# Decoder layer in Winograd's seven products: sums of weight blocks made in other stages

## The chip, the cores and the metric

The kernel runs on one core of a Trainium2 chip. The metric is the time of one execution in microseconds (us) on the device; the kernel before was timed three times.

## The reference

One layer on a residual stream `h` of 1024 tokens by 1024 channels, float32, with `D_FF` = 2816:

```python
f = (silu(n(h) @ w_gate) * (n(h) @ w_up)) @ w_down      # FFN1
h = h + 0.5 * n(f)
z = n(h) @ w_in                                          # u | v | c | ga | gb, 1024 columns each
a = gelu(u) * spatial(layernorm(gelu(v)))                # 128-token chunks, 4 groups
b = pool_mixer(c)                                        # trailing means over 2, 4, 8, 16 tokens
y = sigmoid(ga) * (a @ w_out_a) + sigmoid(gb) * (b @ w_out_b)
h = h + n(y @ w_o)
h = h + 0.5 * n(FFN2(n(h)))                              # like FFN1
h = h + n(sigmoid(n(h) @ ple_w_gate) * (p @ ple_w_proj))
```

`n` is an RMSNorm with a gain of its own at each place.

## The kernel before

Every large product is done in Winograd's form of Strassen's scheme: each operand is cut into 2 by 2 blocks, and seven block products replace eight. They come in the order p1, p2, p5, p6, p3, p7, p4 (`ORDER`), which the text numbers 0 to 6. p1 and p2 use plain blocks of the right operand (the weights), p3 too; p5, p6, p7 and p4 use sums of its blocks (b11+b12 and three more). Each float32 operand is split into a rounded high part (ScalarE, L148) and the rest (VectorE, L149), and three matmuls of 128x512 make one float32 product (L156 to L158). TensorE (PE) therefore works through a fixed list of matmuls, with VectorE (DVE) and ScalarE (ACT) splitting, adding and reading out beside it.

The stages are: projection of p; FFN1 gate and up ("hidden", 11 column groups, `Columns`); FFN1 down (`ffn_down`); v (`Rows`); u and c (`Columns`, 4 groups); the gates with the pool mixer; the products with w_out_a and w_out_b; the product with w_o (`Rows`); FFN2 hidden; FFN2 down; the ple product. A right operand either makes its sums when they are wanted (`from_blocks`, L152: VectorE adds of 128x1024 in `raw` tiles) or reads sums that an earlier stage left in DRAM (`from_stored`).

A down stage has for each of its seven products six steps, written (i, kp) with i the product and kp 0 to 5: five of two 128-row chunks and one of a single chunk, 24 matmuls per full step. A step loads two `raw` tiles of 512 KB and splits them into an `X` tile; loads run three steps ahead. At the end of a product each of four PSUM banks is read out (`outs[t].read`), and from product 4 on `closing` turns the finished tokens into the next stage's left operand: multiply by the gain (L742), add the residual (L754), normalise (L179), transpose on TensorE (L233), split and add (L208 to L216). Tokens come in eight tiles; the transposes of tiles 4 to 7 (T4 to T7 in the text) stand among the first matmuls of the next stage.

Steps that are not urgent wait in `later`, a queue sorted by a key: each readout allows it some us of work. The tile framework then fixes one order of instructions per engine, which the chip keeps; loads and stores of all kinds go through the one queue of SyncE (SP), in order, and an issue whose buffer is not free holds up all behind it. Tile pools that matter: `raw` 6, `f` (`full`) 11, `X` 7, `wt` 4 buffers of 128x1024 or larger.

Before the change, `weight_sums` gives six steps to FFN1 down as `beside`: the sums of w_out_a (two halves), w_out_b (two) and w_o (two). One half is four loads of 512 KB into `f` tiles, four adds of 128x1024 (L152) and four stores (`store_sums`, L416). They are entered in this line of `ffn_down`:

```python
if beside and (kp == 1 or (i, kp) == (0, 3)):
    beside.pop(0)()
```

FFN1 hidden has `row_sums` of the v columns of `w_in` beside groups 3 to 6, FFN2 hidden those of `ple_w_gate`: per quarter two loads of 512 KB, four adds of 128x512, four stores of 256 KB. FFN2 hidden makes its own weight sums for all 11 groups; groups 0 and 1 lead (`lead` 2), so that p1 and p2 of both come before p5 of group 0.

Of the kernel before, what the change touches and what calls it, by code (L numbers as in the profile page):

```python
# [13 lines left out]
P = 128  # L14
T = 1024
D = 1024
# [4 lines left out]
HC = NC // 2  # L21
HT = 512
# [61 lines left out]
def layer_kernel(ctx: ExitStack, tc: tile.TileContext, a: dict, out: bass.AP):  # L84
    nc = tc.nc
    x, p = a["x"][0], a["p"][0, 0]
# [13 lines left out]
    later = Later()  # L100
# [12 lines left out]
    def full(shape=(D,), dt=F32):  # L113

        return fp.tile([P, *shape], dt, name="f", tag="f")
# [11 lines left out]
    def scratch(name, n, w=D):  # L127
        return [dr.tile([P, w], F32, name=f"{name}{i}", tag=f"{name}{i}") for i in range(n)]
# [3 lines left out]
    ga_d, gb_d, y_d = (dr.tile([P, KD, T], F32, name=s, tag=s) for s in ("ga_d", "gb_d", "y_d"))  # L132
    as_d, bs_d = (scratch(s, 7, KD // 2 * HT) for s in ("a_s", "b_s"))

    tr_d = {s: [scratch(f"{s}_t{h}", 4) for h in range(2)] for s in ("w_v", "ple_w_gate")}
    tw_d = {s: [scratch(f"{s}_t{h}", 4) for h in range(2)] for s in ("w_out_a", "w_out_b", "w_o")}
    ws_d = dr.tile([P, HT], F32, name="ws_d", tag="ws_d")
    sv_d = dr.tile([P, KD, T], F32, name="sv_d", tag="sv_d")
    s_d = {s: scratch(f"{s}_s", 7, HC * HT) for s in ("ffn1", "ffn2")}
    t_d = {s: {i: scratch(f"{s}_t{i}", 1, HC * HT)[0] for i in (2, 3, 5, 6)} for s in ("ffn1", "ffn2")}  # L140
# [10 lines left out]
    def add(dst, u, v, e=nc.vector):  # L151
        e.tensor_tensor(dst, u, v, op=ALU.add)  # L152
# [213 lines left out]
    def from_blocks(block, put):  # L366


        def each(u, v):
            for x, y in zip(u, v):  # L370
                add(x, x, y, nc.vector)

        def make(i, st, keep):
            name = ORDER[i][0]
            if name in ("p1", "p2"):
                b = block(i, 0)
                if keep[i]:
                    st[("11", "21")[i]] = b
                return put(b)
            if name == "p5":  # L380
                st["11"] = st.get("11") or block(0, 0)
                st["12"] = block(0, 1)
                each(st["11"], st["12"])
                return put(st["11"])
            if name == "p6":
                st["22"] = block(1, 1)
                each(st["11"], st["22"])
                return put(st["11"])
            if name == "p3":
                return put(st["22"])  # L390
            if name == "p7":
                each(st["12"], st["22"])
                return put(st["12"])
            each(st["11"], st.get("21") or block(1, 0))
            return put(st["11"])

        return make

    def from_stored(block, put, sums):


        def make(i, st, keep):
            where = {"p1": (0, 0), "p2": (1, 0), "p3": (1, 1)}
            name = ORDER[i][0]
            return put(block(*where[name]) if name in where else sums(("p5", "p6", "p7", "p4").index(name)))

        return make

    def store_sums(blocks, dst):

        b11, b12, b22, b21 = (full() for _ in range(4))
        for t, load in zip((b11, b12, b22, b21), blocks):
            load(t)
        for d, t, u, v in ((0, b11, b11, b12), (2, b12, b12, b22), (1, b22, b11, b22), (3, b21, b22, b21)):
            add(t, u, v)
            nc.sync.dma_start(dst[d], t)  # L416
# [4 lines left out]
    class Columns:  # L421
        def __init__(self, groups, blocks, lead, stored=None):


            self.lead = lead
            self.steps = [(g, i) for g in range(lead) for i in range(2)]
            self.steps += [(g, i) for g in range(groups) for i in range(2 if g < lead else 0, 7)]
            state = {}

            def make(step):  # L430
                g, i = step

                def block(r, c):
                    t = raw([4, 256])
                    (w0, *c0), (w1, *c1) = blocks(g)

                    def rows(w):
                        return w[r * HT:(r + 1) * HT, :].rearrange("(k p) f -> p k f", p=P)

                    if w0 is w1 and c1[c] == c0[c] + 1:  # L440
                        nc.sync.dma_start(t, rows(w0)[:, :, c0[c] * P:(c0[c] + 2) * P])
                    else:
                        for n, (w, b) in enumerate(((w0, c0[c]), (w1, c1[c]))):
                            nc.sync.dma_start(t[:, :, n * P:(n + 1) * P], rows(w)[:, :, b * P:(b + 1) * P])
                    return [t]

                def put(b):
                    w = wt([2, 4, 256])
                    split(w[:, 0], w[:, 1], b[0])
                    return w  # L450

                def sums(j):
                    t = raw([4, 256])
                    nc.sync.dma_start(t, stored[g][j].rearrange("p (k f) -> p k f", k=4))
                    return [t]

                f = from_stored(block, put, sums) if stored else from_blocks(block, put)
                return f(i, state.setdefault(g, {}), (g >= lead, g >= lead))

            self.right = Right(make, self.steps, lambda s: LOOK if s < 2 * lead - 1 else 3)  # L460
# [125 lines left out]
        later.add(0, 1.4, second)  # L586


    def hidden_weights(s):
        wg, wu = (a[f"{s}_w_{n}"][0] for n in ("gate", "up"))  # L590
        return Columns(HC, lambda c: ((wg, c, c + HC), (wu, c, c + HC)), 2)

    def row_sums(w, dst):

# [99 lines left out]
    def ffn_down(right, outs, last, beside=()):  # L694

        beside = list(beside)
        for i, (name, place, fresh) in enumerate(ORDER):
            if fresh:
                for t in range(4):
                    outs[t].b[place] = bank()  # L700
            def mm(t, o, k, first, last):
                cols = slice(t * P, (t + 1) * P)
                mm3(
                    outs[t].b[place], (o[:, 0, 0, k, cols], o[:, 0, 1, k, cols]),
                    (o[:, 1, 0, k, :], o[:, 1, 1, k, :]), fresh and first, last,
                )

            outer = PAIRS - TAIL
            for kp in range(outer):
                o, n = right.get(i * PAIRS + kp)  # L710
                for k in range(n):
                    for t in range(4):
                        mm(t, o, k, kp == 0 and k == 0, False)
                    later.allow(2.0)
                if beside and (kp == 1 or (i, kp) == (0, 3)):
                    beside.pop(0)()

            rest = [right.get(i * PAIRS + kp) for kp in range(outer, PAIRS)]
            if i == 6:
                last()  # L720
            for t in range(4):
                for j, (o, n) in enumerate(rest):
                    for k in range(n):
                        mm(t, o, k, False, j == TAIL - 1 and k == n - 1)
                outs[t].read(name)
                later.allow(2.0)
# [45 lines left out]

    w_in = a["w_in"][0]
    h1_cols = hidden_weights("ffn1")


# [51 lines left out]
    left = Seven()  # L828
# [15 lines left out]
    g = gain(a["ffn1_pre_g"][0])  # L844
# [5 lines left out]
    for j in range(2):  # L850
        for t in range(NT):
# [10 lines left out]
            if t % 2 == 1 and len(xs) < NT:  # L862
                n = len(xs)
# [3 lines left out]
    while len(xs) < NT:  # L867
        n = len(xs)
# [4 lines left out]

    def weight_sums():

        steps = []
        for s, dst in tw_d.items():
            w = a[s][0]
            for h in range(2):
                def blocks(w=w, h=h, by_columns=s != "w_o"):  # L880
                    def load(r, c):
                        if by_columns:
                            v = w[r * HT:(r + 1) * HT, c * HT + h * 256:c * HT + (h + 1) * 256]
                            k = 4
                        else:
                            v = w[r * HT + h * 256:r * HT + (h + 1) * 256, c * HT:(c + 1) * HT]
                            k = 2
                        return lambda t: nc.sync.dma_start(
                            t.rearrange("p (k f) -> p k f", k=k), v.rearrange("(k p) f -> p k f", p=P)
                        )  # L890

                    return [load(0, 0), load(0, 1), load(1, 1), load(1, 0)]

                steps.append(lambda blocks=blocks, d=dst[h]: store_sums(blocks(), d))
        return steps

    down = down_weights("ffn1")
    ffn_hidden("ffn1", left, h1_cols, lambda: down.ahead(3), row_sums(w_in[:, D:2 * D], tr_d["w_v"]))
    v_rows = Rows(w_in[:, D:2 * D], tr_d["w_v"])
    left = Seven()  # L900
    ffn_down(
# [100 lines left out]
        u_places, c_places = pairs(), pairs()  # L1002
        return [Out(u_final, u_places), Out(c_final, c_places)]

    uc_cols.run(left, uc_outs, lambda g: None, lambda i: gate_cols.right.ahead(2) if i == 6 else None, 5)
    later.flush()

    def col_pairs(s):
# [140 lines left out]
        if i < 2:  # L1149
            ysum.put(i, slice(2, 4), ALL, o)  # L1150

    o_rows = Rows(a["w_o"][0], tw_d["w_o"])

    def last_a(i):
        if i >= 2:
# [15 lines left out]
    later.add(0, 3.7, lambda: ysum.sums(slice(2, 4), ALL, *(tops[i] for i in range(4)), full((2, HT)), 1.3))  # L1171


    h2_cols = hidden_weights("ffn2")
    left = Seven()
    o_rows.run(
        ysum, closing(1.0, lambda t: h1_d[t], h2_d, "mix_post_g", "ffn2_pre_g", left),
# [86 lines left out]
```

## Time and profile before

| | us |
|---|---|
| three runs | 2123.2, 2124.75 (median), 2127.16 |
| the profiled execution, its own time | 2126.75 |
| its span, first to last instruction | 2125.0 |
| TensorE busy | 2064.4 (97% of the span) |
| VectorE, ScalarE, GpSimd busy | 1473.6, 939.2, 140.4 |

The span is almost all TensorE time, so the places to read are the few where TensorE stands still. In the rows below a timeline line gives the start, the length, engine, source line and operation, tiles written and read, the number of instructions merged, and in brackets the idle time before it and what ended it. A line number is one of the kernel before.

### The profile page before, as it was taken

How to read it: one execution, taken by the hardware profiler on the slowest of the kernel's cores; microseconds unless marked ns; L12 is line 12 of the kernel's file. 1: busy time of each engine (PE TensorE's matmuls, PEld its weight loads, DVE VectorE, ACT ScalarE, POOL GpSimd, SP SyncE). 2: the span in 40 equal slices, each digit the busy share in tenths (PEclk: the TensorE clock that was granted, in tenths of full speed). 3: DMA queues.
4: the chain of work that ended last, by engine and by line, in shares of the span. 5: the costliest groups of instructions: out<-in, count | busy, mean ns of one | idle time of the engine just before them, and what ended most of it. 6: DMA issues, size and time to landing. Idle time of an engine off the chain costs nothing. (4 is left out here: it accounts for less than half of the span.)

```text
span 2125.0 us, 25592 instructions
## 1 busy us (share of the span) xinstructions
PE 2064.4 (97%) x9228; PEld 1707.8 (80%) x9228; DVE 1473.6 (69%) x1789; ACT 939.2 (44%) x1360; POOL 140.4 (7%) x212
## 2 busy tenths in 40 slices
PE   7999999999999899999999999989999999999987
PEld 6888888888887788888788887768888888888876
DVE  6766677677657887568587758896666667454787
ACT  7533333344445643334455535653333334443664
POOL 2000000000011110000000002310000000000222
PEclk9999999999999999999999999999999999999999
DMA  8455756489859325535379985636366556764763
GB/s 292 125 172 174 245 175 217 146 310 405 309 196 346 125 82 179 178 129 182 129 261 363 315 255 204 197 104 208 129 222 234 183 186 233 249 205 146 263 237 129
DMA packets 306289, 448.42 MB, mean 211 GB/s; under 512 B 20593, under 2 KB 177265, under 8 KB 306161
## 3 DMA queue, kind: packets, MB, share of 16 engines
q1 hardware_dynamic: 305072, 444.68, 61.0%
q0 software_dynamic: 1088, 2.10, 0.6%
q8 instruction: 73, 1.20, 0.2%
q14 instruction: 56, 0.45, 0.1%
HBM read 301.21 MB, written 145.49 MB: 210 GB/s over the span
## 5 line engine op out<-in xcount | busy, mean ns | idle before, releaser
L156 PE MATMUL ps<-X,wt 128*128 128x512 f32 x1904 | 742.1, 390 | 2.8 <-DVE wt L149 1.7
L157 PE MATMUL ps<-X,wt 128*128 128x512 f32 x1904 | 742.1, 390 | 0.1
L158 PE MATMUL ps<-X,wt 128*128 128x512 f32 x1904 | 741.0, 390 | 0.0
L149 DVE TENSOR_TENSOR wt<-raw,wt 128x1024 fp32r<-128x1024 f32 x282 | 343.9, 1221 | 221.2 <-ACT wt L148 208.2
L156 PEld LDWEIGHTS ps<-X,wt 128*128 128x128 f32 x1904 | 358.6, 188 | 78.4 <-DVE wt L149 2.2
L158 PEld LDWEIGHTS ps<-X,wt 128*128 128x128 f32 x1904 | 358.2, 188 | 74.9
L157 PEld LDWEIGHTS ps<-X,wt 128*128 128x128 f32 x1904 | 358.5, 188 | 74.1 <-DVE X L149 0.4
L148 ACT CAST wt<-raw 128x1024 fp32r<-128x1024 f32 x282 | 295.6, 1049 | 261.9 <-PE ps L158 125.7
L149 DVE TENSOR_TENSOR X<-raw,X 128x1024 fp32r<-128x1024 f32 (+1 forms) x201 | 223.9, 1145 | 107.1 <-ACT X L148 106.6
L148 ACT CAST X<-raw 128x1024 fp32r<-128x1024 f32 (+1 forms) x201 | 191.8, 994 | 149.6 <-PE ps L158 77.3
L157 PE MATMUL ps<-X 128*128 128x512 f32 x616 | 241.4, 392 | 0.3 <-DVE X L149 0.3
L156 PE MATMUL ps<-X 128*128 128x512 f32 x616 | 237.3, 391 | 3.9 <-ACT X L148 2.7
L158 PE MATMUL ps<-X 128*128 128x512 f32 x616 | 240.0, 391 | 0.0
L152 DVE TENSOR_TENSOR raw<-raw 128x1024 f32<-128x1024 f32 x120 | 146.6, 1222 | 8.1 <-DMA raw<-in_ffn_w_up_dram 3.6
L156 PEld LDWEIGHTS ps<-X 128*128 128x128 f32 x616 | 116.0, 188 | 28.6 <-ACT X L148 3.1
L157 PEld LDWEIGHTS ps<-X 128*128 128x128 f32 x616 | 116.3, 189 | 24.9 <-DVE X L149 0.8
L158 PEld LDWEIGHTS ps<-X 128*128 128x128 f32 x616 | 116.3, 189 | 23.9
L157 PE MATMUL ps<-wt,X 128*128 128x512 f32 x336 | 132.6, 395 | 1.2 <-DVE wt L149 1.2
L158 PE MATMUL ps<-wt,X 128*128 128x512 f32 x336 | 132.1, 393 | 0.0
L156 PE MATMUL ps<-wt,X 128*128 128x512 f32 x336 | 132.0, 396 | 0.0
L341 ACT ACTIVATE f<-ps 128x512 f32<-128x512 f32 x88 | 52.6, 598 | 125.7 <-PE ps L158 125.6
L339 ACT ACTIVATE f<-ps 128x512 f32<-128x512 f32 x88 | 52.2, 596 | 111.3 <-PE ps L158 111.1
(137 smaller groups left out, 1875.5 us busy)
## 6 DMA issues: line engine op xcount, KB each, us to landing
raw<-ffn_s SPq DMA_DIRECT2D x70, 512.0 KB, 5.1
raw<-in_ffn_w_gate_dram SPq DMA_DIRECT2D x96, 256.0 KB, 4.0
raw<-in_ffn_w_up_dram SPq DMA_DIRECT2D x96, 256.0 KB, 4.5
f<-in_ffn_w_down_dram SPq DMA_DIRECT2D x44, 512.0 KB, 4.6
ffn_s<-hf SPq DMA_DIRECT2D x88, 256.0 KB, 3.4
ffn_t<-hf SPq DMA_DIRECT2D x88, 256.0 KB, 4.5
raw<-ffn_t SPq DMA_DIRECT2D x40, 512.0 KB, 5.3
ffn_s<-f SPq DMA_DIRECT2D x66, 256.0 KB, 2.1
```

Source lines behind the costliest of these rows:

```text
L148: nc.scalar.copy(hi, src)
L149: e.tensor_tensor(lo, src, hi.bitcast(F32), op=ALU.subtract)
L152: e.tensor_tensor(dst, u, v, op=ALU.add)
L156: nc.tensor.matmul(ps, wl[1], wr[0], start=first, stop=False, skip_group_check=True)
L157: nc.tensor.matmul(ps, wl[0], wr[1], start=False, stop=False, skip_group_check=True)
L158: nc.tensor.matmul(ps, wl[0], wr[0], start=False, stop=last, skip_group_check=True)
L339: nc.scalar.activation(at("22"), y, AF.Copy, scale=-1.0)
L341: nc.scalar.activation(at("12"), x, AF.Copy, scale=-1.0)
```

## The change

The sums of w_o leave FFN1 down. They become `row_sums` (the form that v has) beside FFN1 hidden, after those of v: groups 7 to 10. FFN1 down keeps the four steps of w_out_a and w_out_b, at kp 1 and 3 of products 0 and 1. The four sums of groups 0 and 1 of FFN2's gate and up weights are made in the stage of u and c by a new function `first_sums`: after each of its four groups eight loads of 128 KB, four adds of 128x512, four stores of 256 KB. FFN2 hidden reads them for its groups 0 and 1 (`from_stored`) and makes sums for the others as before. The list of matmuls is the same.

```diff
-    tr_d = {s: [scratch(f"{s}_t{h}", 4) for h in range(2)] for s in ("w_v", "ple_w_gate")}
-    tw_d = {s: [scratch(f"{s}_t{h}", 4) for h in range(2)] for s in ("w_out_a", "w_out_b", "w_o")}
+    tr_d = {s: [scratch(f"{s}_t{h}", 4) for h in range(2)] for s in ("w_v", "w_o", "ple_w_gate")}
+    tw_d = {s: [scratch(f"{s}_t{h}", 4) for h in range(2)] for s in ("w_out_a", "w_out_b")}
     ws_d = dr.tile([P, HT], F32, name="ws_d", tag="ws_d")
+    tf_d = [scratch(f"ffn2_first{g}_t", 4) for g in range(2)]
...
-                f = from_stored(block, put, sums) if stored else from_blocks(block, put)
+                f = from_stored(block, put, sums) if stored and g < len(stored) else from_blocks(block, put)
...
-                if beside and (kp == 1 or (i, kp) == (0, 3)):
+                if beside and i < 2 and kp % 2 == 1:
                     beside.pop(0)()
...
-    ffn_hidden("ffn1", left, h1_cols, lambda: down.ahead(3), row_sums(w_in[:, D:2 * D], tr_d["w_v"]))
+    ffn_hidden("ffn1", left, h1_cols, lambda: down.ahead(3), row_sums(w_in[:, D:2 * D], tr_d["w_v"]) + row_sums(a["w_o"][0], tr_d["w_o"]))
...
-    uc_cols.run(left, uc_outs, lambda g: None, lambda i: gate_cols.right.ahead(2) if i == 6 else None, 5)
+    def first_sums(g, kk):
+
+        ws = [a[f"ffn2_w_{n}"][0] for n in ("gate", "up")]
+
+        def loaded():
+            tiles = [full((2, 2, 256)) for _ in range(2)]
+            for r, c in ((0, 0), (0, 1), (1, 0), (1, 1)):
+                for n, w in enumerate(ws):
+                    r0, b = r * HT + kk * 256, g + c * HC
+                    rows = w[r0:r0 + 256, b * P:(b + 1) * P].rearrange("(k p) f -> p k f", p=P)
+                    nc.sync.dma_start(tiles[r][:, c, :, n * P:(n + 1) * P], rows)
+
+            def sums():
+                b11, b12, b21, b22 = (t[:, c] for t in tiles for c in range(2))
+                for d, t, u, v in ((0, b11, b11, b12), (2, b12, b12, b22), (1, b22, b11, b22), (3, b21, b22, b21)):
+                    add(t, u, v)
+                    cols = slice(kk * HT, (kk + 1) * HT)
+                    nc.sync.dma_start(tf_d[g][d][:, cols].rearrange("p (k f) -> p k f", k=2), t)
+
+            later.add(93, 2.8, sums, 2)
+
+        later.add(92, 0.0, loaded)
+
+    uc_cols.run(left, uc_outs, lambda g: first_sums(g // 2, g % 2), lambda i: gate_cols.right.ahead(2) if i == 6 else None, 5)
...
-    o_rows = Rows(a["w_o"][0], tw_d["w_o"])
+    o_rows = Rows(a["w_o"][0], tr_d["w_o"])
...
-    h2_cols = hidden_weights("ffn2")
+    h2_cols = hidden_weights("ffn2", tf_d)
```

Three places of VectorE's order, of before and then of the change (whose line numbers are higher by one: L149 is L150, L152 is L153). `X<-raw` is a split of a down step, `f<-f,ps` a readout.

Place A, FFN1 down, the passage from product 5 to product 6. Before (the `f<-f` rows of 128x1024 are sums of w_o, L346 is the readout of product 5):

```order
L149 TENSOR_TENSOR X<-raw,X 128x1024
L152 TENSOR_TENSOR f<-f 128x1024 x3
L346 TENSOR_TENSOR f<-f,ps 128x512 x2
L152 TENSOR_TENSOR f<-f 128x1024
L346 TENSOR_TENSOR f<-f,ps 128x512
L149 TENSOR_TENSOR X<-raw,X 128x1024
L346 TENSOR_TENSOR f<-f,ps 128x512
```

After the change, at the same place:

```order
L150 TENSOR_TENSOR X<-raw,X 128x1024
L150 TENSOR_TENSOR X<-ps,X 128x4x128 x2
L150 TENSOR_TENSOR X<-raw,X 128x1024
L150 TENSOR_TENSOR X<-ps,X 128x4x128 x2
L347 TENSOR_TENSOR f<-f,ps 128x512
L150 TENSOR_TENSOR X<-raw,X 128x1024 x2
L347 TENSOR_TENSOR f<-f,ps 128x512
```

The four sums of w_o are gone from between the splits and the readouts, and the splits of transposed tokens (`X<-ps`) of tiles 2 and 3 stand there, which came later before. From step (3, 3) to the last split of product 6 this order is now row for row that of FFN2 down.

Place B, FFN1 down, the passage from product 1 to product 2. Before (`f<-f,ps` at L152 is the readout of product 1; the first row holds the splits of (2, 0) and half of (2, 1)):

```order
L149 TENSOR_TENSOR X<-raw,X 128x1024 x3
L152 TENSOR_TENSOR f<-f 128x1024
L149 TENSOR_TENSOR X<-raw,X 128x1024 x3
L152 TENSOR_TENSOR f<-f 128x1024
L152 TENSOR_TENSOR f<-f,ps 128x512
L152 TENSOR_TENSOR f<-f 128x1024
L152 TENSOR_TENSOR f<-f,ps 128x512
L742 TENSOR_TENSOR f<-f 128x512
```

After the change (the first row holds the splits of (2, 0) and (2, 1), the third those of (2, 2), the fifth those of (2, 3)):

```order
L150 TENSOR_TENSOR X<-raw,X 128x1024 x4
L153 TENSOR_TENSOR f<-f,ps 128x512 x4
L150 TENSOR_TENSOR X<-raw,X 128x1024 x2
L153 TENSOR_TENSOR f<-f 128x1024 x3
L150 TENSOR_TENSOR X<-raw,X 128x1024 x2
L153 TENSOR_TENSOR f<-f 128x1024
L150 TENSOR_TENSOR X<-raw,X 128x1024 x2
```

The splits of (2, 2) stood ahead of the readouts of product 1 and now stand behind all four, and three sums of w_out_b stand ahead of the splits of (2, 3).

Place C, the start of FFN2 hidden, from the normalisation of token tile 5 to that of tile 6 (`L179 raw<-f,sc`). Before (`L152 raw<-raw` are weight sums of FFN2):

```order
L179 SCALAR_TENSOR_TENSOR raw<-f,sc 128x1024
L152 TENSOR_TENSOR raw<-raw 128x1024
L149 TENSOR_TENSOR X<-ps,X 128x4x128
L213 SCALAR_TENSOR_TENSOR X<-f,X 128x4x128
L742 TENSOR_TENSOR f<-ps,f 128x512
L215 SCALAR_TENSOR_TENSOR f<-f,X 128x512
...
L152 TENSOR_TENSOR f<-f,ps 128x512
L152 TENSOR_TENSOR raw<-raw 128x1024
L179 SCALAR_TENSOR_TENSOR raw<-f,sc 128x1024
```

After the change:

```order
L180 SCALAR_TENSOR_TENSOR raw<-f,sc 128x1024
L150 TENSOR_TENSOR X<-ps,X 128x4x128
L214 SCALAR_TENSOR_TENSOR X<-f,X 128x4x128
L743 TENSOR_TENSOR f<-ps,f 128x512
L216 SCALAR_TENSOR_TENSOR f<-f,X 128x512
...
L153 TENSOR_TENSOR f<-f,ps 128x512
L180 SCALAR_TENSOR_TENSOR raw<-f,sc 128x1024
```

The weight sums are gone from between the two normalisations, and nothing takes their place; the rows left out are the same in both.

## Rows read from the trace of the kernel before

**Rows 1.** The page: span, TensorE's busy time, and from its list of DMA issues one load (count, KB each, median us from issue to landing).

```profile
span 2125.0 us, 25592 instructions
...
PE 2064.4 (97%) x9228; PEld 1707.8 (80%) x9228; DVE 1473.6 (69%) x1789; ACT 939.2 (44%) x1360; POOL 140.4 (7%) x212
...
raw<-in_ffn_w_gate_dram SPq DMA_DIRECT2D x96, 256.0 KB, 4.0
```

**Rows 2.** Who waited for whom, of TensorE: us in total, times, longest us.

```profile
PE ps L233 <- DVE raw L179: 28.2, 11, 5.3
```

**Rows 3.** Timeline of TensorE: rows with idle time before them, in FFN1 down and at the start of FFN2 hidden.

```profile
655.07 0.73 PE L156 MATMUL ps<-X 128*128 128x512 f32 x2 [2.69 <-ACT X L148]
...
656.99 0.79 PE L156 MATMUL ps<-X 128*128 128x512 f32 x1 [1.19 <-DVE f L346]
...
658.13 0.79 PE L157 MATMUL ps<-X 128*128 128x512 f32 x1 [0.34 <-DVE X L149]
...
1372.08 1.40 PE L233 MATMUL ps<-ident,raw 128*128 128x128 f32 x8 [4.35 <-DVE raw L179]
...
1380.94 1.07 PE L233 MATMUL ps<-ident,raw 128*128 128x128 f32 x8 [0.72 <-DVE raw L179]
...
1392.05 1.97 PE L233 MATMUL ps<-ident,raw 128*128 128x128 f32 x8 [4.54 <-DVE raw L179]
...
1403.61 1.94 PE L233 MATMUL ps<-ident,raw 128*128 128x128 f32 x8 [2.85 <-DVE raw L179]
...
1412.95 0.50 PE L156 MATMUL ps<-X,wt 128*128 128x512 f32 x1 [1.04 <-DVE f L152]
```

**Rows 4.** Stretches: length, then busy us (and instructions) of PE, weight loads, DVE, ACT, POOL, granted clock (1.00 is full), share of the DMA engines, GB/s. The first two run from the first matmul of a down stage (FFN1, FFN2) to T7 behind it. The other three run from T4 to T7: at the start of FFN2 hidden, of v, of the ple product.

```profile
465.48:718.72 253.24, 241.36 (x1078) 198.55 (x1076) 174.16 (x187) 120.51 (x179) 28.14 (x40) 0.98 0.82 302
1805.19:2050.76 245.57, 238.08 (x1078) 196.93 (x1076) 144.98 (x161) 119.58 (x179) 28.18 (x41) 1.00 0.66 224
1372.08:1403.61 31.53, 23.41 (x96) 18.87 (x97) 28.68 (x36) 18.75 (x34) 11.70 (x12) 0.83 0.47 151
692.32:718.72 26.40, 19.44 (x97) 15.82 (x97) 25.14 (x35) 18.51 (x33) 7.09 (x11) 0.97 0.53 189
2024.49:2050.76 26.27, 19.47 (x97) 15.83 (x97) 24.13 (x33) 18.10 (x33) 7.98 (x12) 0.96 0.86 314
```

**Rows 5.** Timelines just before TensorE's idle time at 655 us: SP's queue, then VectorE, then ScalarE.

```profile
640.19 2.85 SPq L888 DMA_DIRECT2D f<-in_w_o_dram  x3
...
644.41 1.73 SPq L688 DMA_DIRECT2D raw<-ffn_t  x1
...
651.92 4.77 SPq L416 DMA_DIRECT2D w_o_t<-f  x3
...
650.25 1.23 DVE L152 TENSOR_TENSOR f<-f 128x1024 f32<-128x1024 f32 x1 [2.39 <-DMA f<-in_w_o_dram]
652.78 1.23 DVE L152 TENSOR_TENSOR f<-f 128x1024 f32<-128x1024 f32 x1 [1.30 <-DMA f<-in_w_o_dram]
653.93 1.28 DVE L346 TENSOR_TENSOR f<-f,ps 128x512 f32<-128x512 f32 x2
...
653.98 1.04 ACT L148 CAST X<-raw 128x1024 fp32r<-128x1024 f32 x1 [11.94 <-DMA raw<-ffn_t]
```

**Rows 6.** Timeline of VectorE at the start of FFN2 hidden.

```profile
1377.77 1.23 DVE L152 TENSOR_TENSOR raw<-raw 128x1024 f32<-128x1024 f32 x1 [1.94 <-DMA raw<-in_ffn_w_up_dram]
...
1379.51 1.28 DVE L179 SCALAR_TENSOR_TENSOR raw<-f,sc 128x1024 f32<-128x1024 f32 x1
...
1389.58 1.22 DVE L152 TENSOR_TENSOR raw<-raw 128x1024 f32<-128x1024 f32 x1
1390.72 1.28 DVE L179 SCALAR_TENSOR_TENSOR raw<-f,sc 128x1024 f32<-128x1024 f32 x1
```

**Rows 7.** Groups of VectorE's instructions from 1365 to 1420 us: the weight sums (count, busy us, mean ns, idle us before them).

```profile
L152 DVE TENSOR_TENSOR raw<-raw 128x1024 f32<-128x1024 f32 x6 | 7.3, 1221 | 2.5 <-DMA raw<-in_ffn_w_up_dram 2.5
```

**Rows 8.** Timeline of GpSimd: the scalar step ahead of the normalisation of tile 7, at the start of FFN2 hidden and of the ple product.

```profile
1397.99 3.52 POOL L163 TENSOR_SCALAR sc<-sc 128x1 f32<-128x1 f32 x1 [8.17 <-DVE X L208]
...
2046.92 0.19 POOL L163 TENSOR_SCALAR sc<-sc 128x1 f32<-128x1 f32 x1 [5.59 <-DVE X L149]
```

**Rows 9.** Stretches, columns as in rows 4: FFN1 hidden with the sums of v beside it, the first half of FFN1 down, the stage of u and c.

```profile
204.00:360.00 156.00, 156.00 (x690) 129.23 (x689) 106.47 (x133) 52.93 (x71) 0.00 (x0) 1.00 0.62 212
...
440.00:565.00 125.00, 125.00 (x554) 103.52 (x553) 92.84 (x100) 58.19 (x76) 2.37 (x4) 1.00 0.98 366
...
793.00:952.00 159.00, 158.17 (x747) 132.34 (x746) 100.74 (x135) 56.76 (x74) 0.98 (x3) 1.00 0.52 165
```

**Rows 10.** DMA from 440 to 565 us: GB/s in 40 equal slices, the bytes moved, and the loads of w_out_b (KB each, median us to landing).

```profile
GB/s 182 320 381 393 301 408 364 400 407 326 380 386 385 390 416 415 404 414 418 419 422 388 422 390 418 401 417 415 347 253 175 364 364 399 412 418 415 103 292 312
DMA packets 21810, 45.74 MB, mean 366 GB/s; under 512 B 1596, under 2 KB 9788, under 8 KB 21802
...
f<-in_w_out_b_dram SPq DMA_DIRECT2D x8, 512.0 KB, 10.0
```

**Rows 11.** Timeline of VectorE: the first readout of product 1 in FFN1 down.

```profile
524.84 0.69 DVE L152 TENSOR_TENSOR f<-f,ps 128x512 f32<-128x512 f32 x1 [6.46 <-PE ps L158]
```

**Rows 12.** Groups of VectorE's instructions: the 16 sums of v from 204 to 360 us, and the weight splits of the stage of u and c from 793 to 952 us.

```profile
L152 DVE TENSOR_TENSOR f<-f 128x512 f32<-128x512 f32 x16 | 10.9, 683 | 0.0
...
L149 DVE TENSOR_TENSOR wt<-raw,wt 128x1024 fp32r<-128x1024 f32 x28 | 34.2, 1223 | 37.2 <-ACT wt L148 37.2
```

More of the change, by code (lines that the diff above doesn't have):

```diff
@@ L586, in spill, with hidden_weights @@
         later.add(0, 1.4, second)
-    def hidden_weights(s):
+    def hidden_weights(s, stored=None):
         wg, wu = (a[f"{s}_w_{n}"][0] for n in ("gate", "up"))
-        return Columns(HC, lambda c: ((wg, c, c + HC), (wu, c, c + HC)), 2)
+        return Columns(HC, lambda c: ((wg, c, c + HC), (wu, c, c + HC)), 2, stored)
     def row_sums(w, dst):
@@ L874, in weight_sums, with one, load @@
     def weight_sums():
[L876 to L895, printed above, removed]
+        def one(w, h, dst):
+            def load(r, c):
+                v = w[r * HT:(r + 1) * HT, c * HT + h * 256:c * HT + (h + 1) * 256]
+                return lambda t: nc.sync.dma_start(
+                    t.rearrange("p (k f) -> p k f", k=4), v.rearrange("(k p) f -> p k f", p=P)
+                )
+            return lambda: store_sums([load(0, 0), load(0, 1), load(1, 1), load(1, 0)], dst)
+        return [one(a[s][0], h, dst[h]) for s, dst in tw_d.items() for h in range(2)]
     down = down_weights("ffn1")
-    ffn_hidden("ffn1", left, h1_cols, lambda: down.ahead(3), row_sums(w_in[:, D:2 * D], tr_d["w_v"]))
+    ffn_hidden("ffn1", left, h1_cols, lambda: down.ahead(3), row_sums(w_in[:, D:2 * D], tr_d["w_v"]) + row_sums(a["w_o"][0], tr_d["w_o"]))
     v_rows = Rows(w_in[:, D:2 * D], tr_d["w_v"])
```

## The prediction, made before the changed kernel had run

> **What bounds the kernel now.** I read the page first: TensorE is busy 2064.4 of 2125.0 us [rows 1], so only its 60.6 us of idle time, and matmuls that run slower for the same work, can be won. The list of matmuls is the same before and after, so nothing comes off the 2064.4 us but the slow part. Next the list of who waited for whom: the largest wait of TensorE, 28.2 us in 11 waits, is the transposes (L233) waiting for the normalisation L179 on VectorE [rows 2]. Then TensorE's timeline, for the places of these waits that lie where the change works. There are two [rows 3]: the passage from product 5 to 6 of FFN1 down (2.69, 1.19 and 0.34 us, 4.22 in sum) and the start of FFN2 hidden (4.35, 0.72, 4.54, 2.85 and 1.04 us). At 1412.95 the releaser is an L152 add into an `f` tile.
>
> Last, tables of stretches, because this kernel does the same thing in several places and one can stand as the measure of another [rows 4]. FFN1 down from its first matmul to T7 takes 253.24 us, FFN2 down 245.57, both with 1078 matmuls. The 7.67 us are 4.39 of idle time (253.24−241.36 against 245.57−238.08) and 3.28 of longer busy time for the same matmuls, at a granted clock of 0.98 against 1.00. So here an idle us brought 3.28/4.39 = 0.75 us more by the clock: I price an idle us inside a down stage at 1.75 us. From T4 to T7 the start of FFN2 hidden takes 31.53 us, those of v and ple 26.40 and 26.27, at clocks of 0.83, 0.97 and 0.96, for 96 or 97 matmuls.
>
> **The change: sums of w_o leave FFN1 down.** The queue of SP tells why TensorE stood at 655 us. Three loads of w_o go out at 640.19, the load of a down step (`raw<-ffn_t`) has its turn at 644.41 and holds the queue 1.73 us, and three stores of w_o sums at 651.92, where the queue stands 4.77 us [rows 5]. ScalarE's cast of that `raw` tile begins at 653.98 after 11.94 us of waiting for the load; VectorE waits 2.39 and 1.30 us for loads of w_o, with the readouts L346 behind these sums, at 653.93. Both releasers of TensorE's idle time, the cast and the readout, are thus behind w_o. Place A shows what stays: splits and readouts alone, in FFN2 down's order. FFN2 down does not have these stalls, so I take its whole difference: 7.7 us. The lower bound is the idle time alone, 4.2, if the slower clock had another cause; nothing, if the stall is of the `raw` buffers and not of w_o (a rival). I take the upper value since the two stages have the same matmuls, and now the same VectorE order from step (3, 3).
>
> **The change: sums of w_o enter FFN1 hidden.** Sixteen adds of 128x512 with loads and stores, in the form that v has. While v's ran, TensorE was busy 156.00 of 156.00 us and VectorE 106.47 [rows 9]; the 16 adds took 10.9 us with no idle time of VectorE ahead of them [rows 12]. Cost: 0, covered by VectorE's 49.5 free us in such a stretch. If the cover is gone, it is at most the 10.9.
>
> **The change: w_out_a and w_out_b by kp 1 and 3.** The same number of instructions, closer together, the last ones earlier. The critical place is B: the splits of (2, 2) stood ahead of the readouts of product 1, and now wait behind all four, which TensorE paces (the first began at 524.84 after VectorE had waited 6.46 us for it [rows 11]). At the first readout TensorE has two steps, (2, 0) and (2, 1), already split: 48 matmuls of 125.00/554 us [rows 9] are 10.8. Four readouts of 0.69 us [rows 11] take 2.8, so about 8 us of cover is left when the splits of (2, 2) come. The three sums that follow take 1.22 each by the 128x1024 add in [rows 7], 3.7, with the next step's two splits 1.2 each: 6.1 per 5.4 us of TensorE (24 matmuls), which eats under 1 us of it: 7.5 left. Cost: 0.
>
> Its DMAs: from 440 to 565 us the core moved 45.74 MB at a mean of 366 GB/s [rows 10], with a DMA share of 0.98 [rows 9]. Both halves of w_out_b were already loaded there (8 loads of 512 KB) [rows 10]; the change adds at its front up to the last two quarters of w_o, each two loads of 512 KB and four stores of 256 KB, 4.2 MB in all. The slices reach 422 GB/s [rows 10]. At 422, 49.9 MB take 118 us and fit into the 125; at the mean, 136.4 us, which is 11.4 late. I take it as fitting, since the late loads are issued ahead and the slices above 400 follow each other; the other value is rival B.
>
> The Trainium skill (DMA: Bandwidth & Descriptors, Specifications) names about 358 GB/s as the limit of a core from HBM; by that figure the stretch would take 139.5 us (an estimate), 14.5 late, and the sum would be 2123 by B's working. Slices of 400 to 422 GB/s in this trace [rows 10] disagree with it as a ceiling.
>
> **The change: weight sums of FFN2 groups 0 and 1.** What goes away: six L152 adds between 1365 and 1420 us, 7.3 us busy with 2.5 of waiting for their loads [rows 7]. They stand right ahead of L179 (1377.77 before 1379.51, with 1.94 of wait; 1389.58 before 1390.72) [rows 6], and L179 is what T5 and T6 wait for [rows 3]. T4's own 4.35 is ahead of all of them and stays. Without them this start is like that of v and ple, which have a normalisation chain but no such sums: 31.53−26.3 = 5.2 [rows 4], and the 1.04 at 1412.95, behind an L152 too, 6.2 in sum. Bounds: below, the one DMA wait and the 1.04, 3.0; above, all the idle time from T5 on, 9.15, and the busy excess 23.41−19.44 = 3.97 [rows 4], 13.1. I take 6.2, nearest the two twins.
>
> What it costs: 16 adds of 128x512 in the stage of u and c, 0.683 us each, 10.9 [rows 12]. There VectorE stood idle 37.2 us ahead of its 28 weight splits [rows 12], and TensorE 0.83 us in all [rows 9]; DMA was at 0.52 [rows 9]. Cost: 0, by that idle time. At the passage to the gates the last four adds stand in the same stretch as the pool mixer. If the cover is gone there, the four adds (2.7) and a load's landing of 4.0 [rows 1] fall on TensorE: 6.7. The new loads of the stored sums in FFN2 hidden take the place of more bytes of weights: nothing.
>
> **The sum.** 7.7 + 6.2 = 13.9. The profiled execution, 2126.75 (span 2125.0 and 1.75 around it), becomes 2112.85; it lay 2.0 above the median of 2124.75, so by the median 2110.85, about 2111.
>
> **Rivals.**
>
> *B. DMA limits products 1 and 2 of FFN1 down.* For it: the 0.98 share; against: the slices up to 422. Loads 11.4 late less the 7.5 of cover are 3.9 of idle time, by 1.75 6.8: 2117.7.
>
> *C. The passage from u and c to the gates loses its cover.* For it: the last adds and their loads stand with the mixer; against: the 37.2 free us. +6.7: 2117.6.
>
> *D. The start of FFN2 hidden doesn't become faster,* since another chain sets T7. For it: the scalar step of GpSimd (L163) ahead of T7's normalisation took 3.52 us here and 0.19 at ple [rows 8], and its wait ended on a VectorE split. Against: T5 and T6 wait for L179 with sums right ahead of it. 2124.75−7.7 = 2117.0. The Trainium skill (GPSIMD Engine Reference, 8. Key points) has GpSimd and VectorE contend for their shared SBUF interfaces when VectorE reads two inputs there; by that the 3.52 would shrink with the adds gone, and no row shows it alone.
>
> *E. The stall at 655 stays,* the `raw` buffers being its cause: only 6.2 is won, 2118.5. For it: the step's load waited for its turn; against: SP's queue stood 4.77 us on stores of w_o.
>
> *F. Slower:* at place B the cover is gone, because the splits of (2, 2) wait behind readouts and three sums, and the loads are late by the full 11.4. By 1.75 that is 19.9, less 13.9: +6.0, 2130.8. It decides from 13.9/1.75 = 7.9 us of new idle time on. Against: two steps split ahead.
>
> **How the numbers follow.** 0.2% (4.25 us) is about what a measurement of this kernel can tell from no change. Chances: forecast 0.60, B 0.07, C 0.08, D 0.05, E 0.05, two of these four together 0.08 (13.9−6.7−6.8, within 0.2%), F 0.07. Each of B to E alone ends 6 to 8 below the median, close enough to the limit that I count 0.03 of their 0.25 as within it. Faster 0.82, same 0.11, slower 0.07. The bounds of the two gains give 2124.75−20.8 = 2104 and 2124.75−7.2 = 2117.5 for the forecast; both ends together are unlikely, and its own range is 2106 to 2116. The range of all reaches over B to E to 2120 and leaves out the pairs and F.
>
> **What would show it right or wrong.** In FFN1 down: no idle time at the start of product 6, first matmul to T7 near 245.6 us, and no `raw` cast that waits near 12 us. Wrong, if TensorE stands in products 1 to 3 instead (a split L150 or a cast as releaser, a load behind it). In FFN2 hidden: no L153 `raw<-raw` add between T4 and T7, that stretch near 26.3 us at a clock near 0.96; wrong, if L180 still releases T6 and T7 by over 2 us each. In FFN1 hidden and in u and c: TensorE without idle time beside the new adds, and none at the first gate product beyond before. T4's 4.35 stays.

## The result and the profile after

The changed kernel takes 2113.17 us (median; 2111.83 to 2116.65), the kernel before beside it 2125.38: 12.2 us less, ratio 0.994, interval 0.9928 to 0.9952. A second timing gave 2114.21 against 2127.09, 12.9 us less, with the same ratio. The forecast was 2111, in a range of 2106 to 2120, and 13.9 us less.

The page after, its lines that answer to [rows 1]:

```profile
span 2110.1 us, 25680 instructions
...
PE 2054.8 (97%) x9228; PEld 1701.8 (81%) x9228; DVE 1472.8 (70%) x1805; ACT 938.1 (44%) x1360; POOL 132.7 (6%) x212
```

The span is 14.9 us shorter (the profiled execution before lay above its median, this one below). With the same 9228 matmuls 9.6 us come off TensorE's busy time and 5.3 off its idle time. In the first 50 us, though, before anything that the change moves, the waits of this execution happen to sum to 2.67 us more (15.39 against 12.72). Behind 60 us, 7.0 come off the busy time and 7.9 off the idle time: the same matmuls running faster give nearly as much as the waits themselves.

The stretches of [rows 4] again: FFN1 down and FFN2 down from the first matmul to T7, then T4 to T7 at the start of FFN2 hidden (columns as there):

```profile
465.82:711.53 245.71, 238.10 (x1077) 196.95 (x1075) 168.99 (x186) 119.16 (x178) 25.38 (x40) 0.99 0.79 290
1791.02:2036.59 245.57, 238.07 (x1077) 196.95 (x1075) 144.99 (x161) 119.56 (x179) 28.15 (x41) 1.00 0.65 224
1364.86:1391.05 26.19, 20.83 (x96) 17.12 (x97) 24.15 (x32) 18.52 (x33) 9.11 (x12) 0.95 0.57 195
```

FFN1 down (253.24 us before) is now as long as FFN2 down, within 0.14 us, and the start of FFN2 hidden went from 31.53 to 26.19 us. TensorE's timeline, waits over 0.15 us from FFN1 down to T7 of FFN2 hidden, answers to [rows 3]:

```profile
685.12 1.06 PE L234 MATMUL ps<-ident,raw 128*128 128x128 f32 x8 [0.70 <-DVE raw L180]
...
711.53 1.97 PE L234 MATMUL ps<-ident,raw 128*128 128x128 f32 x8 [5.26 <-DVE raw L180]
797.15 0.33 PE L157 MATMUL ps<-f,raw 128*128 128x128 f32 x1 [0.78 <-DVE raw L938]
1038.52 0.50 PE L157 MATMUL ps<-X,wt 128*128 128x512 f32 x1 [1.75 <-DVE wt L150]
1115.17 0.50 PE L157 MATMUL ps<-X,wt 128*128 128x512 f32 x1 [0.20 <-DVE f L347]
1291.48 0.50 PE L158 MATMUL ps<-wt,X 128*128 128x512 f32 x1 [1.02 <-DVE wt L150]
1302.83 0.50 PE L158 MATMUL ps<-wt,X 128*128 128x512 f32 x1 [0.16 <-DVE wt L150]
1364.86 1.97 PE L234 MATMUL ps<-ident,raw 128*128 128x128 f32 x8 [4.60 <-DVE raw L180]
1380.62 1.09 PE L234 MATMUL ps<-ident,raw 128*128 128x128 f32 x8 [1.50 <-DVE raw L180]
1391.05 1.42 PE L234 MATMUL ps<-ident,raw 128*128 128x128 f32 x8 [3.86 <-DVE raw L180]
```

Nothing is left at product 6 of FFN1 down. At the start of FFN2 hidden T5's wait of 0.72 us is gone and T6's falls from 4.54 to 1.50; T4's grows from 4.35 to 4.60 and T7's from 2.85 to 3.86. At 1115 there is a small wait that the kernel before did not have.

### The profile page after: what moved, and what is told of

It reads as the page before. It is cut to its first block, busy times and chain, and to the rows that moved or that the text cites. A ratio compares the mean times of both kernels' runs of the same rounds, so it can differ in the third digit from the quotient of the medians.

```text
span 2110.1 us, 25680 instructions
## 1 busy us (share of the span) xinstructions
PE 2054.8 (97%) x9228; PEld 1701.8 (81%) x9228; DVE 1472.8 (70%) x1805; ACT 938.1 (44%) x1360; POOL 132.7 (6%) x212
## 5 line engine op out<-in xcount | busy, mean ns | idle before, releaser
L150 DVE TENSOR_TENSOR wt<-raw,wt 128x1024 fp32r<-128x1024 f32 x282 | 344.4, 1223 | 199.5 <-ACT wt L149 182.1
L149 ACT CAST wt<-raw 128x1024 fp32r<-128x1024 f32 x282 | 295.6, 1050 | 260.8 <-PE ps L159 127.9
L150 DVE TENSOR_TENSOR X<-raw,X 128x1024 fp32r<-128x1024 f32 (+1 forms) x201 | 224.2, 1148 | 112.7 <-ACT X L149 112.2
L149 ACT CAST X<-raw 128x1024 fp32r<-128x1024 f32 (+1 forms) x201 | 191.6, 993 | 131.1 <-PE ps L159 54.5
L153 DVE TENSOR_TENSOR raw<-raw 128x1024 f32<-128x1024 f32 x112 | 137.0, 1223 | 5.9 <-DMA raw<-in_w_in_dram 2.4
```

The costliest lines, as they stand in the source:

```text
L149: nc.scalar.copy(hi, src)
L150: e.tensor_tensor(lo, src, hi.bitcast(F32), op=ALU.subtract)
```

## The experiments

Where two runs are compared below, each is taken by its difference to the kernel before beside it: 2126.97 us in the first group (parts of the change), 2127.09 in the second and 2127.25 in the third.

### Each part alone

The part on w_o alone:

```diff
-    uc_cols.run(left, uc_outs, lambda g: first_sums(g // 2, g % 2), lambda i: ...
+    uc_cols.run(left, uc_outs, lambda g: None, lambda i: ...
-    h2_cols = hidden_weights("ffn2", tf_d)
+    h2_cols = hidden_weights("ffn2")
```

> The change without the sums for FFN2: w_o beside FFN1 hidden, w_out_a and w_out_b at kp 1 and 3 of products 0 and 1, FFN2 hidden makes all its sums itself. Theory (the stall of FFN1 down is of w_o, priced by FFN2 down): 7.7 us under before, about 2117.7, first matmul of FFN1 down to T7 near 245.6 to 247, and from T4 to T7 at the start of FFN2 hidden still 31.5 us. Rival 'idle time alone' (the slower clock has another cause): 4.2 us, about 2121.2. Rival 'the two parts only work together': under 3 us.

2118.70 us: 8.3 less, ratio 0.9962 (0.9949 to 0.9976). The theory holds on both counts (FFN1 down from its first matmul to T7 takes 245.71 us, T4 to T7 31.62); the rival "idle time alone" (4.2) does not. The `raw` buffers are the same and the stall at 655 is gone, so rival E of the prediction falls too.

The part on FFN2 alone: the change with `weight_sums`, its entry line and `o_rows` as before.

> The kernel before with only the sums of FFN2's groups 0 and 1 moved to the stage of u and c. Theory: 6.2 us under before, about 2119.2, with T4 to T7 at FFN2's start near 26.3, and the passage from product 5 to 6 of FFN1 down with its 4.2 us of idle time as before. Rival C (the sums cost cover where u and c pass to the gates): no gain, 2125, with TensorE idle near the first gate products. Rival D (another chain sets T7): within 2 us of before, T4 to T7 still above 30.

2118.24 us: 8.7 less, ratio 0.9959 (0.9946 to 0.9971), 2.5 more than the theory said; C and D fall. From T4 to T7 at the start of FFN2 hidden, with w_o alone:

```profile
1365.35:1396.97 31.62, 24.85 (x97) 20.23 (x97) 29.39 (x37) 18.66 (x33) 10.56 (x12) 0.80 0.46 149
```

and with the sums for FFN2 alone:

```profile
1373.56:1398.25 24.69, 21.15 (x97) 17.19 (x97) 23.36 (x31) 18.69 (x33) 6.80 (x12) 0.93 0.61 209
```

Each part acts where it should. But 8.3 and 8.7 make 17.0, and the change brings 12.2 to 12.9:

> The change itself again, on the chip and beside the kernel before as the other runs of this call, to see whether its two parts add up. Theory (they touch different places): the sum of the two parts run alone, which lay 8.3 and 8.7 us under before, so 17 us under, ratio 0.992. Rival (they share something, such as the clock or the stall at FFN2's start that each run shows differently): 12 to 14 us under, ratio 0.994, as in the first timing.

2114.21 us, 12.9 less: the rival. The profiles show part of the gap. T4 to T7 at the start of FFN2 hidden takes 24.69 us with one part and 26.19 with both, 1.5 more (see the last section). From T7 to the first matmul of FFN2 down the parts alone win 1.17 (w_o) and 2.15 us (FFN2), the change 1.61 and, in its second timing, 0.72; why is open. And at 1115 TensorE waits for a readout which stands on VectorE behind a split that waits for a load of `a_s`: 1.75 us in the profile of this second timing, 0.20 in the first, none before or with the sums for FFN2 alone. With w_o alone it is 0.78, so it can be at most 1.0 us of the gap, and none of it in the first timing. It comes with w_o's move: of the eight other kernels below that have w_o beside FFN1 hidden, all but one show it. Why that load is late is open. The intervals (about 2.8 us to each side) leave room for the rest.

### Was it lateness, or w_o in FFN1 down at all?

```diff
-                if beside and (kp == 1 or (i, kp) == (0, 3)):
+                if beside and i < 3 and kp % 2 == 1:
```

> The kernel before with all six steps of weight sums kept in FFN1 down, but entered at kp 1 and 3 of products 0, 1 and 2, so that SP's queue holds the last store of w_o before the loads of product 5. Theory 'w_o was too late, just ahead of the passage to product 6': the stall goes as in the run that moves w_o to FFN1 hidden, 7 to 8 us under before, about 2117.7. Rival 'the DMA engines of FFN1 down have no room for six steps': the stall moves to products 1 to 4, gain under 4 us, above 2121, with TensorE idle there behind a load.

2129.54 us: 2.6 more than before, ratio 1.0014 (1.0005 to 1.0023). The stall at 655 is gone, and a larger one stands two products earlier, at the passage from product 3 to 4. TensorE's timeline there:

```profile
594.92 0.50 PE L158 MATMUL ps<-X 128*128 128x512 f32 x1 [0.99 <-DVE X L150]
597.19 0.50 PE L158 MATMUL ps<-X 128*128 128x512 f32 x1 [0.58 <-DVE X L150]
600.81 0.77 PE L157 MATMUL ps<-X 128*128 128x512 f32 x1 [2.19 <-DVE X L150]
602.98 0.80 PE L158 MATMUL ps<-X 128*128 128x512 f32 x1 [1.41 <-DVE X L150]
```

The stretch (columns of [rows 4]):

```profile
592.00:604.00 12.00, 6.57 (x21) 3.84 (x20) 11.97 (x12) 9.39 (x12) 0.00 (x0) 0.87 0.85 282
```

VectorE's timeline:

```profile
587.29 1.23 DVE L150 TENSOR_TENSOR X<-raw,X 128x1024 fp32r<-128x1024 f32 x1 [16.76 <-ACT X L149]
...
592.51 1.22 DVE L153 TENSOR_TENSOR f<-f 128x1024 f32<-128x1024 f32 x1
...
597.05 2.47 DVE L153 TENSOR_TENSOR f<-f 128x1024 f32<-128x1024 f32 x2
...
600.58 1.22 DVE L153 TENSOR_TENSOR f<-f 128x1024 f32<-128x1024 f32 x1
```

VectorE stood 16.76 us for a cast; then it had splits and four sums to do at once, busy 11.97 of 12.00 us, and TensorE waited for the splits. So an earlier place in the stage does not help, as my theory had it; this passage holds no room for w_o either. My rival named the wrong engine: here it is the cast's place behind the readouts in ScalarE's order and then VectorE, not the DMA queue, whose share is 0.85. The run also gives a price: the waits sum to 5.43 us with one more of 0.26, and FFN1 down from its first matmul to T7 takes 255.05 us where it takes 245.71 in the change. That is 9.34 us, at a clock of 0.87 in the stretch above: 1.72 us per idle us, where I had 1.75 from the two down stages.

### The other half of the first edit: where w_out is entered

w_o moves, but the entry line of `ffn_down` is as before.

> w_o beside FFN1 hidden, but w_out_a and w_out_b entered where they were before (kp 1 of products 0 to 2 and kp 3 of product 0); no sums for FFN2. Theory (front-loading of w_out costs and brings nothing): the same as the run with kp 1 and 3 within 1.5 us, about 2117.7. Rival B (front-loading presses on the DMA queue of products 1 and 2): this one is 2 us or more faster than that run.

2119.67 us, 7.3 less against 8.3: within 1.5, and FFN1 down takes 245.71 us from its first matmul to T7 in both. Front-loading costs nothing, and B falls.

### What about w_o made the stall: transfers or adds?

Two kernels have w_o beside FFN1 hidden and do part of w_o's old work at its old entries in FFN1 down once more.

```diff
+        for t, load in zip((b11, b12, b22, b21), blocks):
+            load(t)
+        for d, t in ((0, b11), (2, b12), (1, b22), (3, b21)):
+            nc.sync.dma_start(dst[d], t)
```

> As the run with w_o beside FFN1 hidden and w_out entered as before (7.3 us under before), but FFN1 down again has w_o's eight loads and eight stores at the old entries, without the adds (what they store is not read). No sums for FFN2. Theory 'the stall at 655 is of the transfers' (they fill SP's queue and the DMA engines, and the loads of the down steps land late): most of the 7.7 us comes back, about 2125, with TensorE idle near product 6 behind a cast that waits for a load. Rival 'VectorE's adds ahead of the readouts make it': it stays near 2119.

2123.10 us, 4.0 less than before: 3.3 of the 7.3 us come back, between theory and rival. TensorE waits 0.79, 0.70 and 0.64 us at product 6, and FFN1 down to T7 takes 248.74 us, 3.03 more than without w_o.

The second has the loads and the adds (`add(t, u, v)` in the place of the stores):

> As the run with w_o's transfers alone in FFN1 down, but with w_o's eight loads and eight adds at the old entries and without the eight stores (what is added is not read). VectorE's order at the passage to product 6 is that of the kernel before: three sums ahead of the first readout, one behind it. The transfers without adds brought back 3.4 of the 7.5 us. Theory 'the adds carry the rest': with them and half the transfers it is near the kernel before, 2124 to 2126, with 4 us of idle time there. Rival 'transfers alone': with half of them it is 1 to 2 us above the run without w_o in FFN1 down, about 2121.

2119.84 us, 7.4 less: nothing comes back, and TensorE does not wait at product 6 (FFN1 down to T7: 246.14 us), although VectorE has three sums ahead of the first readout, as before, and one behind it. My theory falls. What differs is how fast the loads land. DMA issues around the passage (KB each, median us from issue to landing): first before (636 to 660 us):

```profile
w_o_t<-f SPq DMA_DIRECT2D x6, 512.0 KB, 8.6
f<-in_w_o_dram SPq DMA_DIRECT2D x5, 512.0 KB, 7.6
...
raw<-ffn_t SPq DMA_DIRECT2D x3, 512.0 KB, 9.5
```

With loads and stores (636 to 660 us):

```profile
raw<-ffn_t SPq DMA_DIRECT2D x4, 512.0 KB, 6.4
w_o_t<-f SPq DMA_DIRECT2D x3, 512.0 KB, 8.1
f<-in_w_o_dram SPq DMA_DIRECT2D x2, 512.0 KB, 8.7
```

With loads and adds (638 to 662 us):

```profile
f<-in_w_o_dram SPq DMA_DIRECT2D x5, 512.0 KB, 5.1
raw<-ffn_t SPq DMA_DIRECT2D x5, 512.0 KB, 5.5
```

The loads of the kind that the cast waits for take 9.5 us in the median before, 6.4 with the transfers alone, 5.5 without the stores. So the stores are needed for the stall, and the adds do not hold TensorE by their own time. Transfers alone bring back 3.3 of the 7.3 us; the other 4 come only with adds and stores together. With the adds the stores come bunched (six in these 24 us before, three without adds), which is my reading of those 4 us and was not tried by itself. Why the load lands late is open too. The DMA engines do not run at their top rate when it goes out, at 644.41: from 641 to 647 us they move only 109 to 249 GB/s, and over 420 in slices before and behind.

### What made the start of FFN2 hidden slow: adds or loads?

```diff
-            for x, y in zip(u, v):
+            for x, y in zip(u, v) if summed else ():
```

> As the run of the w_o part alone, but FFN2 hidden leaves out the adds of groups 0 and 1 (their products take unsummed blocks, so the result differs) and keeps all their loads; no sums in the stage of u and c. Theory (VectorE's adds ahead of the normalisations make T5 to T7 late): as with the whole change, 5 to 6 us under the w_o part alone, about 2113, T4 to T7 near 26.3. Rival 'the loads do it' (wait of 1.94 us for a load, DMA): under 2 us of gain, about 2117.

2114.45 us, 12.6 less than before and 4.4 less than w_o alone; T4 to T7:

```profile
1364.57:1390.99 26.42, 21.09 (x97) 17.13 (x97) 24.30 (x32) 19.18 (x36) 8.61 (x12) 0.90 0.55 179
```

The adds are the cause: with their loads still there the stretch is within 0.23 us of the change's 26.19.

### What is left there

> The change, and in FFN2 hidden three groups lead instead of two: p1 and p2 of three groups come before p5 of group 0, so that T4 to T7 stand among six products instead of four. What is left of idle time there is the latency of the normalisation chain, not VectorE's load, by my reading of the trace of the change (waits 4.60, 1.50 and 3.86 us ahead of T4, T6 and T7). If so, T6 and T7 find other matmuls ahead of them: 3 to 5 us under the change, ratio near 0.992. Rival: the third group's own sums, loads and banks press on VectorE there: no gain or slower than the change.

2114.65 us, 12.4 less: no gain over the change. T4 to T7 keep their places in TensorE's order, and T7 still waits 3.87 us. So they were moved as well (`late` 1, and 2 in the run after):

```diff
-            left.feed(hp, t, t + 2, max(3, t))
+            left.feed(hp, t, t + 2, max(3, t) + (late if t >= 4 else 0))
...
-        return Columns(HC, lambda c: ((wg, c, c + HC), (wu, c, c + HC)), 2, stored)
+        return Columns(HC, lambda c: ((wg, c, c + HC), (wu, c, c + HC)), 3 if stored else 2, stored)
```

> The change with three leading groups in FFN2 hidden, and the transposes T4 to T7 there entered one readout (24 matmuls) later each. Three leading groups alone left T4's 4.40 and T7's 3.87 us of idle time as they were, since the transposes kept their places 0, 24, 48 and 72 matmuls into the stage. Theory: with 24 matmuls (5.4 us) more ahead of each, these waits go, 8 us of idle time and the slower clock behind it: 8 to 11 us under the change, ratio about 0.990. Rival: the splits behind T7 come too late for p5 of group 0 and TensorE stands there instead: no gain.

2109.55 us, 17.7 less than before, ratio 0.9917 (0.9904 to 0.9931): 4.8 under the change, where I expected 8 to 11. Not all waits went: T4's is 1.67 us, T5's 1.20 and T6's 3.50; T7 has none.

> As the run before in this call, with the transposes two readouts (48 matmuls) later than in the change. Theory: the waits are covered already with one; T7 at 120 of 144 matmuls leaves 24 matmuls for its splits ahead of p5, so the same or 1 to 3 us slower than with one. Rival 'the more the better': faster.

2106.98 us, 20.3 less, ratio 0.9904 (0.989 to 0.9918): faster than both kernels, and better than I expected of the second step, though its interval overlaps that of the first. Waits of TensorE at this start with `late` 2; the one ahead of T4 is gone:

```profile
1380.65 1.09 PE L234 MATMUL ps<-ident,raw 128*128 128x128 f32 x8 [2.02 <-DVE raw L180]
1390.79 1.97 PE L234 MATMUL ps<-ident,raw 128*128 128x128 f32 x8 [3.20 <-DVE raw L180]
```

> The change with two leading groups as it has, and T4 to T7 one readout later: T7 at 96 matmuls, right ahead of p5 of group 0, whose operand needs its splits. Theory: the idle time ahead of T4 and T7 goes, but comes back ahead of p5: within 2 us of the change. Rival: the splits are quick and 4 us or more are won without a third group.

2115.53 us, 11.7 less, within 2 us of the change. T4's wait falls to 1.58 us and T7's goes, 6.88 in all, but 7.48 come back ahead of T5, T6 and p5:

```profile
1363.55 1.06 PE L234 MATMUL ps<-ident,raw 128*128 128x128 f32 x8 [1.58 <-DVE raw L180]
1371.32 1.09 PE L234 MATMUL ps<-ident,raw 128*128 128x128 f32 x8 [1.20 <-DVE raw L180]
1381.38 1.09 PE L234 MATMUL ps<-ident,raw 128*128 128x128 f32 x8 [3.50 <-DVE raw L180]
...
1395.54 0.74 PE L157 MATMUL ps<-X,wt 128*128 128x512 f32 x2 [2.39 <-ACT X L149]
1398.16 0.80 PE L158 MATMUL ps<-X,wt 128*128 128x512 f32 x1 [1.89 <-DVE X L150]
```

Both are needed: the later place, and a third group whose matmuls stand between T7 and p5. With `late` 2 T7's wait goes only from 3.86 to 3.20 with 48 matmuls more ahead of it: its normalisation moves back nearly as far, by my reading because VectorE and GpSimd do other work first; that was not tried.

## Why the prediction was right, and where not

**FFN1 down, 7.7 us.** First matmul to T7 became 7.53 us shorter (253.24 to 245.71), and up to the wait at 797 us (804.97 before) the kernel won 8.16 from the first matmul on, which comes 0.34 later. The twin stage was the right measure: the idle time alone would have given 4.2. The 7.53 us for 4.22 of idle time are 1.78 per idle us, where I had 1.75. In all nine profiles without w_o in FFN1 down, first matmul to T7 takes 245.71 to 245.73 us. Right in size, and the cast that waited for its load was the right releaser. The step that failed is the cause given for the other releaser, the readout "behind these sums": with the sums in place and the stores gone there is no stall. Nor can the 4.77 us that SP's queue stands at 651.92, which the prediction holds against rival E, have delayed that load: it went out ahead of them, at 644.41, and the cast began 9.6 us later [rows 5]. The place was right that w_o sits on, the mechanism half right.

**Start of FFN2 hidden, 6.2 us.** T4 to T7 gave 5.34 (forecast 5.2). Behind T7, up to T4 of the ple product, the kernel is another 1.61 us shorter, where I had the 1.04 of the wait at 1412.95. Less 0.25 by which T4's own wait grew. The sums were what stood ahead of T5 and T6, as argued, and the twins v and ple gave the total. In part that is luck: the 26.19 us are made up otherwise than v's 26.40, with 20.83 us busy and 5.36 idle where v has 19.44 and 6.96. Of the sign of being wrong, "over 2 us each" at T6 and T7, T7's half came: its wait grew by 1.01.

**Costs taken as nothing.** FFN1 hidden: none. From the wait at 797.15, over the stage of u and c and the passage to the gates, to the next wait at 1038.52 it is 241.37 us; before, from 804.97 to 1046.34, it was 241.37 too. That next wait is 1.75 us in both; C did not come. Place B, VectorE's timeline:

```profile
525.18 0.69 DVE L153 TENSOR_TENSOR f<-f,ps 128x512 f32<-128x512 f32 x1 [8.91 <-PE ps L159]
...
531.30 0.69 DVE L153 TENSOR_TENSOR f<-f,ps 128x512 f32<-128x512 f32 x1 [1.35 <-PE ps L159]
531.91 2.36 DVE L150 TENSOR_TENSOR X<-raw,X 128x1024 fp32r<-128x1024 f32 x2
534.18 3.74 DVE L153 TENSOR_TENSOR f<-f 128x1024 f32<-128x1024 f32 x3
537.83 2.35 DVE L150 TENSOR_TENSOR X<-raw,X 128x1024 fp32r<-128x1024 f32 x2
```

Product 2 begins when product 1's last readout can, about 531.3, and has 48 matmuls ready, 10.8 us, until 542.1. The splits of (2, 2) end at 534.3: 7.8 us of cover. I had 8, but ahead of those splits and counted from the first readout, as if the four came in a row; they come 2.04 us apart, each when TensorE is done with its bank, and ahead of the splits there are 10.2. That the two figures are alike is luck. B and F did not come: TensorE was busy 125.00 of 125.00 us from 440 to 565 while the DMA engines moved more than before:

```profile
440.00:565.00 125.00, 125.00 (x553) 103.56 (x552) 88.86 (x97) 51.67 (x68) 1.52 (x4) 1.00 1.01 375
```

That is 46.9 MB, not the 49.9 that I had counted: six loads of down steps fewer fall into these 125 us than before. So the rate that the 49.9 needed was not tried, and what the run shows is only that no load came late enough to stop TensorE. The mean is 375 GB/s, loads and stores together. The Trainium skill's limit of about 358 GB/s from HBM (DMA: Bandwidth & Descriptors, Specifications) disagrees with this as a ceiling, as it did with the slices of [rows 10].

**What the sum left out.** The wait at 1115, 0.2 to 1.75 us, was in no term; and I took the gains as additive, which the runs of the parts don't bear out (17.0 alone, 12.2 to 12.9 together). The 13.9 came out close to the 12.2 to 12.9 measured. The terms above are read from two profiled executions that lie 14.9 us apart, more than the medians do, so the last us or two of them is not settled.

**Rival D** was wrong: the start did become faster. What it pointed at is still there, a slow scalar step of GpSimd ahead of T7 (2.38 us, 3.52 before), but it is a small part of T7's 3.86 us, as the last section shows.

## To carry to other kernels

Where a kernel does the same stage twice, the stage without the stall is a good price for the stall: it holds the clock's share too, which the idle time alone leaves out. Background work in a busy stage is priced by what it does to the landing time of the loads that the passages wait for, and by its adds only where VectorE is full at a passage; where it moves to, look for passages first. A wait for a long chain is moved away only if the waiting instruction goes later and other matmuls are put ahead of what depends on it; one without the other won nothing here.

## What was not expected of the hardware

A scalar step of GpSimd on 128x1 took 2.38 us ahead of T7 in the change and 0.52 with the sums for FFN2 alone. GpSimd's timeline in the change:

```profile
1386.57 2.38 POOL L164 TENSOR_SCALAR sc<-sc 128x1 f32<-128x1 f32 x1 [7.03 <-DVE X L209]
```

VectorE beside it:

```profile
1386.41 0.69 DVE L650 TENSOR_TENSOR f<-f 128x512 f32<-128x512 f32 x1
...
1388.21 0.70 DVE L150 TENSOR_TENSOR X<-X 128x512 fp32r<-128x512 f32 x1
1389.62 1.28 DVE L180 SCALAR_TENSOR_TENSOR raw<-f,sc 128x1024 f32<-128x1024 f32 x1 [0.71 <-POOL sc L165]
```

GpSimd's timeline with the sums for FFN2 alone:

```profile
1394.13 0.52 POOL L164 TENSOR_SCALAR sc<-sc 128x1 f32<-128x1 f32 x1 [5.67 <-ACT raw L170]
```

The slow step ends at 1388.95, as VectorE's run of four instructions with two inputs in SBUF ends (1388.91), and VectorE then waits 0.71 us for what follows on it. With w_o alone the step takes 2.92 us and ends at 1394.87, VectorE's run at 1394.82; in the kernel before 3.52, 1401.51 and 1401.46. The Trainium skill (GPSIMD Engine Reference, 8. Key points) says that the two engines contend for shared SBUF interfaces in such instructions; these rows and the 3.52 against 0.19 of [rows 8] agree, though no run here changed VectorE's instructions alone to show it.

It is not what makes the start of FFN2 hidden 1.5 us longer with both parts than with one: VectorE loses at most those 0.71 us to it. The 1.5 lie between T6 and T7, 10.43 us with both (1380.62 to 1391.05) and 8.92 with the sums alone (1389.33 to 1398.25), and there VectorE's order differs. VectorE's timeline with both, where a split of weights stands ahead of the residual add (L755) of T7's tokens:

```profile
1382.88 1.22 DVE L150 TENSOR_TENSOR wt<-raw,wt 128x1024 fp32r<-128x1024 f32 x1
1384.01 1.29 DVE L755 SCALAR_TENSOR_TENSOR f<-f,sc,raw 128x1024 f32<-128x1024 f32 x1
```

and with the sums for FFN2 alone, where it stands behind:

```profile
1391.58 1.27 DVE L755 SCALAR_TENSOR_TENSOR f<-f,sc,raw 128x1024 f32<-128x1024 f32 x1
1392.78 1.21 DVE L150 TENSOR_TENSOR wt<-raw,wt 128x1024 fp32r<-128x1024 f32 x1
```

The add begins 3.39 us behind T6 with both and 2.25 with the sums alone: 1.14 of the 1.5 us come ahead of GpSimd's step. No run changed that place by itself.
